# Gate projections in 1024-column blocks, part of them by seven products instead of eight

## The chip, the cores and the metric

The kernel runs on one core of one Trainium2 chip. The metric is the device time of one execution in microseconds (us). TensorE multiplies matrices, VectorE (DVE in the profile) and ScalarE (ACT) work element by element, SyncE (SP) issues the loads and stores; each engine takes its instructions in a fixed order, and they wait for one another by semaphores.

## The reference, cut

One layer of a transformer block for 256 rows of width 2048: three kinds of attention, each with its own branch projection, gates on the branches, an output projection, and a feed-forward part with a short convolution.

```python
h = rms_norm(x, g_mix[l])
proj = h @ w_in[l]
fq, fk, fv, f_logit, sq, sk, sv, mq, gates = jnp.split(proj, cuts, axis=-1)
...            # o_fox, o_sb, o_mem: three attentions over 6, 6 and 4 heads of 128
g = jax.nn.sigmoid(gates.reshape(b, s, N_BRANCH, D_MODEL) + b_gate[l])
merged = (g[:, :, 0] * (o_fox @ w_br_fox[l])
          + g[:, :, 1] * (o_sb @ w_br_sb[l])
          + g[:, :, 2] * (o_mem @ w_br_mem[l]))
x = x + merged @ w_out[l]
h2 = rms_norm(x, g_ffn[l])
u = causal_depthwise_conv(h2 @ w_up[l], conv_w[l], conv_b[l])
u_gate, u_val = jnp.split(u, 2, axis=-1)
x = x + (jax.nn.silu(u_gate) * u_val) @ w_down[l]
```

All inputs are float32. The gates are 3 x 2048 of the columns of `w_in`: a product of 256 x 2048 by 2048 x 6144.

## The kernel before

**Numbers in two parts.** Each float32 operand is held as a rounded part "hi" and a rest "lo". A product is three matmuls (`passes`, L151 to L153, and `three`, L277 to L279): hi by hi, lo of the activations by hi of the weights, hi of the activations by lo of the weights. A piece of weights of 128 x 1024 is loaded into a `raw` tile by SP, copied to `hi` by ScalarE (L140, L272) and split into `lo` by VectorE (L141, L273). `raw` has four buffers (`WBUFS`), `hi` and `lo` four each (`SBUFS`), taken in turn.

**Stages, in order.** The memory's keys and values; projections for the three attentions (mq, f0 to f4, s0 to s4) with the heads' work between them; the gates and branches; the output projection (`o`); the up projection with the convolution (`u`); the down projection (`d`).

**Gates and branches.** The loop at L899 runs over four column blocks `n` of 512. In each, the three gates are projected by `proj` (16 k tiles, two per piece; two row tiles; three matmuls: 96 matmuls a gate), scaled and biased by VectorE straight from PSUM (L910) and passed through the sigmoid (L912); then the three branches are projected by `product` and multiplied in (L924 to L927), and `merged_T` (L877) transposes the merged block for the output projection.

**Eight or seven products.** The output and down projections are made in blocks of 1024 columns by `blocked` (L315), in which a pair of k tiles is a 2 x 2 problem (two row tiles, two column halves, two k tiles). `eight` makes its eight products. `seven` makes seven, in Winograd's manner: it needs sums of the activations (`pair_sums`, L281) and sums of the weights, and adds into four banks `X` and four banks `Y`, which `gather` (L296) puts together on VectorE. A plan string says which pair is done how: "e" by eight, "s" by seven, "f" forms sums of activations. The X and Y banks together are all eight PSUM banks.

**Sums of weights.** They don't depend on the activations, and `weight_sums` (L237) makes them ahead in the background, half a pair at a time: two loads into a tile `pre`, three adds on VectorE (L259 to L261), and a store to DRAM (`kept`), from which `seven` loads them ready made. A half starts every `period` calls of `tick` (one per piece of weights). In the first part of the kernel the period is 7, with the store after 5.

```python
background.append(
    weight_sums(lambda name: gp.tile([P, 1024], F32, tag="pre", bufs=1, name=name), 7, 5, "merged")
)
```

**Order.** TensorE's, ScalarE's and VectorE's order comes from a scheduler, apart from what `keep_in_program_order` fixes. `later` puts a generator of head work, transposes or gathering into a queue, and `tick` runs up to two of them a step further. `xres` holds x for the residual; it is read early for the transposed activations `xT` and the row norms, and again when the output projection is added to it (L303 to L313, L971).

## Time and profile before

| | |
|---|---|
| median of 3 runs | 1474.45 us (1474.35 to 1475.05) |
| span of the profiled execution | 1472.5 us, the only time the page gives of it |
| TensorE busy | 1467.2 us (100%) |
| VectorE busy | 1123.3 us (76%) |
| ScalarE busy | 819.1 us (56%) |
| DMA, mean over the span | 249 GB/s, 367.31 MB |

The profile is of one execution. "PE" is TensorE's matmuls, "PEld" its loads of the stationary operand. A row of a group of instructions has line, engine, operation, tiles written and read, shapes and count, then busy time, mean duration of one in ns, and the idle time of the engine just before them with what ended it. A row of the timeline has start and duration in us. A row of DMA issues ends with size and the median time from issue to landing. A row of a stretch has each engine's busy time with its number of instructions, the granted clock of TensorE, the share of the DMA engines and GB/s. Line numbers are those of the kernel before.

### The profile page before, as it was taken

Reading aid. Unit: us, or ns where it says so; the run is one execution under the profiler, and the core shown is the slowest. Engines: PE = TensorE matmul, PEld = TensorE weight load, DVE = VectorE, ACT = ScalarE, POOL = GpSimd, SP = SyncE. Lnnn points to the kernel's source line nnn. Section 1 sums busy time; section 2 is a strip of 40 time slices with the busy share of each in tenths; the row PEclk is TensorE's granted clock in tenths of the full one; section 3 lists DMA queues with packets and bytes.
Section 4 is the critical chain, followed back from the end, with each engine's and each line's share of the span. In section 5 each row is a group of like instructions: output and inputs, shape, how many; then the busy total and the mean of one; then the engine's idle time right before and its main releaser. Section 6 shows DMA issues by size and latency. Waiting matters only on the chain.

```text
span 1472.5 us, 20543 instructions
## 1 busy us (share of the span) xinstructions
PE 1467.2 (100%) x7373; PEld 1244.8 (85%) x7373; DVE 1123.3 (76%) x1698; ACT 819.1 (56%) x1163; POOL 18.1 (1%) x46
## 2 busy tenths in 40 slices
PE   9999999999999999999999999999999999999999
PEld 7888888888888888888888888888888888888887
DVE  5777666667666657776888899888888777997877
ACT  6755454464544344445666556565566565674664
POOL 0000000011000000000000000000000000000000
PEclk9999999999999999999999999999999999999999
DMA  9685686577788788777758888888885666797796
GB/s 311 203 273 178 206 282 220 172 248 231 239 254 266 247 260 259 245 239 262 251 195 267 288 289 283 281 285 285 285 262 185 198 186 201 242 319 270 258 329 225
DMA packets 213428, 367.31 MB, mean 249 GB/s; under 512 B 13498, under 2 KB 81998, under 8 KB 213326
## 3 DMA queue, kind: packets, MB, share of 16 engines
q1 hardware_dynamic: 211998, 363.90, 76.2%
q10 hardware_dynamic: 1328, 2.11, 0.4%
q8 instruction: 57, 0.93, 0.2%
q14 instruction: 45, 0.37, 0.1%
HBM read 333.44 MB, written 32.51 MB: 249 GB/s over the span
## 4 chain that ended last, share of the span: by engine, by line
PE 99%; DMA 0%; SPq 0%; DVE 0%; ACT 0%; issue 0%; DVEq 0%
PE u L1049 22%; PE u L1050 11%; PE g L151 6%; PE g L153 6%; PE g L152 6%; PE xd L277 4%; PE xd L278 4%; PE xd L279 4%; PE s L151 2%; PE s L153 2%; PE f L151 2%; PE f L153 2%; PE s L152 2%; PE f L152 2%; PE b L152 2%; PE b L151 2%
## 5 line engine op out<-in xcount | busy, mean ns | idle before, releaser
L1049 PE MATMUL u<-hT,hi_u 128*128 128x512 f32 x1232 | 428.4, 391 | 0.0
L1050 PE MATMUL u<-hT,lo_u 128*128 128x256 f32 x1232 | 345.0, 280 | 0.0
L1049 PEld LDWEIGHTS u<-hT,hi_u 128*128 128x128 f32 x1232 | 230.4, 187 | 50.5
L141 DVE TENSOR_TENSOR lo_u<-raw_u,hi_u 128x1024 fp32r<-128x1024 f32 x176 | 215.1, 1222 | 73.1 <-ACT hi_u L140 72.3
L140 ACT CAST hi_u<-raw_u 128x1024 fp32r<-128x1024 f32 x176 | 184.9, 1051 | 137.4 <-PE u L1049 121.0
L1050 PEld LDWEIGHTS u<-hT,lo_u 128*128 128x128 f32 x1232 | 232.8, 189 | 0.0
L141 DVE TENSOR_TENSOR lo_g<-raw_g,hi_g 128x1024 fp32r<-128x1024 f32 x96 | 117.3, 1225 | 78.9 <-ACT hi_g L140 78.3
L140 ACT CAST hi_g<-raw_g 128x1024 fp32r<-128x1024 f32 x96 | 101.0, 1053 | 135.4 <-PE g L152 106.9
L151 PE MATMUL g<-hi_g,xT 128*128 128x512 f32 x336 | 132.0, 393 | 0.0
L153 PE MATMUL g<-lo_g,xT 128*128 128x512 f32 x336 | 130.9, 390 | 0.0
L152 PE MATMUL g<-hi_g,xT 128*128 128x512 f32 x336 | 130.8, 389 | 0.0
L273 DVE TENSOR_TENSOR lo_d<-raw_d,hi_d 128x1024 fp32r<-128x1024 f32 x88 | 106.8, 1222 | 21.1 <-ACT hi_d L272 18.2
L272 ACT CAST hi_d<-raw_d 128x1024 fp32r<-128x1024 f32 x88 | 92.0, 1054 | 49.0 <-PE xd L278 21.4
L153 PEld LDWEIGHTS g<-lo_g,xT 128*128 128x128 f32 x336 | 63.1, 188 | 13.4
L152 PEld LDWEIGHTS g<-hi_g,xT 128*128 128x128 f32 x336 | 63.1, 188 | 12.7
L151 PEld LDWEIGHTS g<-hi_g,xT 128*128 128x128 f32 x336 | 63.1, 188 | 12.7
L140 ACT CAST hi_f<-raw_f 128x1024 fp32r<-128x1024 f32 (+1 forms) x40 | 38.6, 967 | 52.6 <-PE f L152 47.6
L141 DVE TENSOR_TENSOR lo_f<-raw_f,hi_f 128x1024 fp32r<-128x1024 f32 (+1 forms) x40 | 44.7, 1119 | 28.5 <-ACT hi_f L140 26.9
L278 PE MATMUL xd<-hi_d,aT 128*128 128x512 f32 x170 | 66.2, 389 | 0.0
L279 PE MATMUL xd<-lo_d,aT 128*128 128x512 f32 x170 | 66.2, 389 | 0.0
L277 PE MATMUL xd<-hi_d,aT 128*128 128x512 f32 x170 | 66.1, 389 | 0.0
L141 DVE TENSOR_TENSOR lo_s<-raw_s,hi_s 128x1024 fp32r<-128x1024 f32 (+1 forms) x40 | 44.9, 1122 | 27.3 <-ACT hi_s L140 25.2
(422 smaller groups left out, 3029.7 us busy)
## 6 DMA issues: line engine op xcount, KB each, us to landing
raw_u<-in_w_up_dram SPq DMA_DIRECT2D x176, 512.0 KB, 4.5
raw_g<-in_w_in_dram SPq DMA_DIRECT2D x96, 512.0 KB, 4.4
raw_d<-in_w_down_dram SPq DMA_DIRECT2D x66, 512.0 KB, 5.5
pre_d<-in_w_down_dram SPq DMA_DIRECT2D x88, 256.0 KB, 4.8
kept_d<-pre_d SPq DMA_DIRECT2D x44, 512.0 KB, 6.2
raw_f<-in_w_in_dram SPq DMA_DIRECT2D x32, 512.0 KB, 4.2
raw_s<-in_w_in_dram SPq DMA_DIRECT2D x32, 512.0 KB, 4.8
raw_o<-in_w_out_dram SPq DMA_DIRECT2D x25, 512.0 KB, 5.8
```

Source lines behind the costliest of these rows:

```text
L140: pin(nc.scalar.copy(hi[:, :m], raw[:, :m]))
L141: pin(nc.vector.tensor_tensor(lo[:, :m], raw[:, :m], hi[:, :m].bitcast(F32), ALU.subtract))
L151: pin(nc.tensor.matmul(o, lhsT=xh, rhs=wh, start=first, stop=False))
L152: pin(nc.tensor.matmul(o, lhsT=xl, rhs=wh, start=False, stop=False))
L153: pin(nc.tensor.matmul(o, lhsT=xh, rhs=wl, start=False, stop=last))
L272: nc.scalar.copy(hi[:, :n], src)
L273: nc.vector.tensor_tensor(lo[:, :n], src, hi[:, :n].bitcast(F32), ALU.subtract)
L277: nc.tensor.matmul(o, lhsT=ah, rhs=w[0], start=first, stop=False)
L278: nc.tensor.matmul(o, lhsT=al, rhs=w[0], start=False, stop=False)
L279: nc.tensor.matmul(o, lhsT=ah, rhs=w[1], start=False, stop=last)
L1049: nc.tensor.matmul(ps[i], lhsT=hi[:, j, c], rhs=hT(k + j), start=first, stop=False)
L1050: nc.tensor.matmul(ps[i][:, :S], lhsT=lo[:, j, c], rhs=hT(k + j)[:, :S], start=False, stop=last)
```

## The change

The gates are made by `blocked`, in two halves `m` of 1024 columns by three branches, six blocks in all. The first is made by eight throughout. In the other five, three of the eight k pairs are made by seven products. The sums of the weights are not kept in DRAM here: `seven_here` makes them in the raw tiles after their own parts are split off, with four adds of 512 columns, and splits the sums in turn. The sums of the activations, `xs`, are formed for three pairs by `x_sums` behind the forget heads; they lie in the place of `xres`, so x is loaded a second time, behind the first branch weights of the second half. In a block with sevens the bias is added when the Y banks are gathered (`gathered`), with `rneg`, the negated row norm, for subtraction. Both column halves of the three gates are made before the branches of that half. The background's weight sums run with period 4 and store after 3 until the first gate block is done, then with 8 and 3. The matmuls of the gate stage are kept in program order. `merged_T` and `merged_sums` yield a step or more less.

```diff
+    g_plans = (("eeeeeeee", "esesesee", "esesesee"), ("eesessee", "esesesee", "esesesee"))
...
-            for _ in range(period - store):
+            for _ in range(period - store + (slower if "heads" in issued else 0)):
                 yield
...
+        def seven_here(p, first, last):
+            raw0, raw1 = load(2 * p), load(2 * p + 1)
+            (B00,) = parts(raw0[:, :512], f"{name}{nb}_{2 * p}")
+            three(Y[0], *a_of(p, 0, 0), B00, first, last)
+            B10, B11 = parts(raw1, f"{name}{nb}_{2 * p + 1}")
+            three(X[0][0], *a_of(p, 1, 0), B10)
+            three(X[0][1], *f_of(p, FS4), B11)
+            b0, b1 = (raw.rearrange("p (n c) -> p n c", n=2) for raw in (raw0, raw1))
+            nc.vector.tensor_tensor(b0[:, 0], b0[:, 0], b0[:, 1], ALU.add)
+            nc.vector.tensor_tensor(b0[:, 1], b0[:, 1], b1[:, 1], ALU.add)
+            tick()
+            T1w, T3w = parts(raw0, f"t_{name}{nb}_{2 * p}")
+            nc.vector.tensor_tensor(b1[:, 1], b1[:, 1], b0[:, 0], ALU.add)
+            nc.vector.tensor_tensor(b1[:, 0], b1[:, 0], b1[:, 1], ALU.add)
+            three(Y[2], *f_of(p, FS1), T1w, first, last)
+            three(Y[3], *f_of(p, FS3), T3w, first, last)
+            T4w, T2w = parts(raw1, f"t_{name}{nb}_{2 * p + 1}")
+            three(X[1][0], *a_of(p, 1, 1), T4w)
+            three(Y[1], *f_of(p, FS2), T2w, first, last)
+            tick()
...
-        weight_sums(lambda name: gp.tile([P, 1024], F32, tag="pre", bufs=1, name=name), 7, 5, "merged")
+        weight_sums(lambda name: gp.tile([P, 1024], F32, tag="pre", bufs=1, name=name), 4, 3, "merged", slower=4)
...
+    xs = cst.tile([P, GS, 4, 2, P], F32R, tag="xres", name="xs")
+    def x_sums():
+        for p in range(GS):
+            pair_sums(xT.pair(p), block(f"xw_{p}"), [(xs[:, p], slice(0, 4))])
+            yield 2
+    later(x_sums())
...
-    for n in range(4):
-        gate = []
-        for b in range(3):
-            bg = gp.tile([P, 512], F32, tag="bg", name=f"bg_{n}_{b}")
-            nc.sync.dma_start(bg, b_gate[0, b, n0 : n0 + 512].partition_broadcast(P))
-            ps = proj(C_GATE + b * D + n0, 512, f"g{n}_{b}")
-            for t in range(NT):
-                nc.vector.scalar_tensor_tensor(g[:, t], ps[t], rstd[:, t : t + 1], bg, ALU.mult, ALU.add)
+    ordered[0] = True
+    for m in range(2):
+        gate = []
+        for b, plan in enumerate(g_plans[m]):
+            def gathered(n0, Y, m=m, b=b, g=g, bias=bias):
+                ...
+                nc.scalar.copy(e, Y[0])
+                scaled(g[0][:, 0], Y[0], rstd[:, 0:1], 0)
+                nc.vector.tensor_tensor(e, e, Y[1], ALU.add)
+                yield
+                nc.vector.tensor_tensor(f, e, Y[2], ALU.add)
+                scaled(g[1][:, 0], f, rneg[:, 0:1], 1)
+                nc.vector.tensor_tensor(f, e, Y[3], ALU.add)
+                scaled(g[0][:, 1], f, rstd[:, 1:2], 0)
+                yield
+                nc.vector.tensor_tensor(f, f, Y[2], ALU.add)
+                scaled(g[1][:, 1], f, rneg[:, 1:2], 1)
+            X = blocked(
+                "g", w_in, f"{m}{b}", C_GATE + b * D + m * PIECE, plan, lambda p, j: xT(2 * p + j),
+                lambda p, f: xs[:, p, f], raw_g, None, gathered, biases,
+            )
+            for n in range(2):
+                for t in range(NT):
+                    add = g[n][:, t] if "s" in plan else bias[n]
+                    nc.vector.scalar_tensor_tensor(g[n][:, t], X[t][n], rstd[:, t : t + 1], add, ALU.mult, ALU.add)
+            issued.add("heads")
...
+                if (m, n, i) == (1, 0, 1):
+                    xres = cst.tile([P, NT, D], F32, tag="xres", name="xres_again")
+                    for t in range(NT):
+                        nc.sync.dma_start(xres[:, t], xv[:, t])
```

In the text below B00 is the split of a seven's first half tile, B1 that of its second tile, T1/T3 and T4/T2 those of the sums that the adds leave in the first and the second tile.

More of the change, by code (lines that the diff above doesn't have):

```diff
@@ L37 @@
 WINDOW = 2
+GS = 3
 @with_exitstack
@@ L235, in hybrid_block, with weight_sums @@
     )
-    def weight_sums(staging, period, store, end=None, delay=0):
+    def weight_sums(staging, period, store, end=None, delay=0, slower=0):
         for _ in range(delay):
@@ L276, in three @@
     def three(o, ah, al, w, first=False, last=False):
-        nc.tensor.matmul(o, lhsT=ah, rhs=w[0], start=first, stop=False)
-        nc.tensor.matmul(o, lhsT=al, rhs=w[0], start=False, stop=False)
-        nc.tensor.matmul(o, lhsT=ah, rhs=w[1], start=False, stop=last)
+        fix = in_order if ordered[0] else lambda ins: ins
+        fix(nc.tensor.matmul(o, lhsT=ah, rhs=w[0], start=first, stop=False))
+        fix(nc.tensor.matmul(o, lhsT=al, rhs=w[0], start=False, stop=False))
+        fix(nc.tensor.matmul(o, lhsT=ah, rhs=w[1], start=False, stop=last))
     def pair_sums(pair, w, groups):
@@ L383, in seven @@
             tick()
+        def seven_here(p, first, last):
[18 more added lines that the diff above has]
+            tick()
+        by_seven = seven if t4_tile else seven_here
         s, e = 0, ns
@@ L404, in hybrid_block @@
     make_identity(nc, ident)
-    xres = cst.tile([P, NT, D], F32, name="xres")
+    xres = cst.tile([P, NT, D], F32, tag="xres", name="xres")
     xv = x[0].rearrange("(t p) d -> p t d", p=P)
@@ L519, in hybrid_block @@
     ssf = cst.tile([P, NT, 4], F32, name="ssf")
+    rneg = cst.tile([P, NT], F32, name="rneg")
     mix = ctx.enter_context(ExitStack())
@@ L966, in hybrid_block @@
     for nb, plan in enumerate(o_plans):
-        X = blocked("o", w_out, nb, plan, lambda p: mT[p], lambda p, f: ms[p][:, f], raw_o, t4_o[nb], block)
+        X = blocked(
+            "o", w_out, nb, nb * PIECE, plan, lambda p, j: mT[p][:, j], lambda p, f: ms[p][:, f], raw_o, t4_o[nb],
+            lambda n0, Y: gather(n0, Y, block),
+        )
         for n in range(2):
```

85 lines of the change are left out of this document (54 added, 31 removed).

## The prediction

> **What bounds the kernel now.** I read the page's totals and its chain first, then the waits of TensorE, then the chain in order of time for the pitch of its matmuls, then stretches of the gate stage, and last VectorE's timeline and the landings of loads.
>
> ```profile
> span 1472.5 us, 20543 instructions
> PE 1467.2 (100%) x7373; PEld 1244.8 (85%) x7373; DVE 1123.3 (76%) x1698; ACT 819.1 (56%) x1163; POOL 18.1 (1%) x46
> PE 99%; DMA 0%; SPq 0%; DVE 0%; ACT 0%; issue 0%; DVEq 0%
> ...
> PE spare L90 <- DVE qscale L447: 1.2, 1, 1.2
> PE kv L152 <- DVE memT L181: 0.4, 1, 0.4
> ...
> 503.91 0.43 PE mt L885 x4
> 507.12 0.44 PE mt L885 x4
> 591.93 0.44 PE mt L885 x4
> ```
>
> TensorE carries 99% of the chain and in the whole run waits twice, 1.6 us together. So a matmul taken away is time gained, as long as TensorE is still fed. Its price is the pitch, not the 0.39 us that a row shows: between the transposes at 503.91 and those at 591.93 lies one column block of gates and branches, 384 matmuls and 8 transposes of some 0.11 us: (88.02 - 0.88) / 384 = 0.227 us.
>
> ```profile
> core 0: us, PE busy (x) PEld busy (x) DVE busy (x) ACT busy (x) POOL busy (x), PEclk, DMA share, GB/s
> 100.00:125.00 25.00, 25.00 (x116) 20.95 (x115) 18.62 (x34) 13.70 (x24) 0.00 (x0) 1.00 0.76 236
> 275.00:300.00 25.00, 25.00 (x141) 21.51 (x141) 16.03 (x24) 11.87 (x19) 1.73 (x4) 1.00 0.44 127
> 425.00:450.00 25.00, 25.00 (x112) 20.71 (x111) 14.88 (x16) 11.03 (x11) 0.00 (x0) 1.00 0.83 264
> 1275.00:1300.00 25.00, 25.00 (x112) 20.70 (x111) 24.97 (x41) 18.57 (x26) 0.00 (x0) 1.00 0.84 279
> ...
> ACT hi_g L140 <- PE g L152: 106.9, 70, 2.2
> ```
>
> In the gate stage (425 to 450) VectorE is busy 14.9 us of 25, and what ScalarE waits for there is TensorE giving a hi buffer back: the weights are made early. The last row shows that a stage with VectorE busy all the time can still keep TensorE fed (products by seven, in the down projection); but there the sums of weights come ready from DRAM and six raw buffers serve, where the new gates have four and make the sums in place.
>
> **What is gained.** Five blocks have three products by seven each; a seven has 21 matmuls where an eight has 24. 15 x 3 = 45 matmuls x 0.227 = 10.2 us. Everything else on TensorE stays.
>
> **What VectorE gets.** Its price is again a pitch:
>
> ```profile
> 597.13 0.41 DVE L288 TENSOR_TENSOR mw<-mw 128x256 f32<-128x256 f32 x1
> 597.47 1.22 DVE L141 TENSOR_TENSOR lo_g<-raw_g,hi_g 128x1024 fp32r<-128x1024 f32 x1
> ...
> 603.17 0.74 DVE L910 SCALAR_TENSOR_TENSOR g<-g,rstd,bg 128x512 f32<-128x512 f32 x1
> 603.83 0.68 DVE L285 TENSOR_TENSOR mw<-mT 128x512 f32<-128x512 f32 x1
> ...
> 609.42 0.42 DVE L288 TENSOR_TENSOR mw<-mw 128x256 f32<-128x256 f32 x1
> 609.88 0.29 DVE L289 SCALAR_TENSOR_TENSOR mw<-mw 128x128 f32<-128x128 f32 x1
> ...
> 712.05 1.22 DVE L273 TENSOR_TENSOR lo_o<-raw_o,hi_o 128x1024 fp32r<-128x1024 f32 x1
> 713.18 0.68 DVE L312 TENSOR_TENSOR e<-e,yo 128x512 f32<-128x512 f32 x1
> 713.78 0.68 DVE L971 TENSOR_TENSOR xres<-xres,xo 128x512 f32<-128x512 f32 x1
> ```
>
> From start to start a split of 1024 columns takes 1.13 us (712.05 to 713.18), an add of 512 takes 0.60, a scaling 0.66 (603.17 to 603.83), an add of 256 takes 0.34; an op that reads the one before it starts 0.04 behind that one's end (609.88 behind 609.42 + 0.42), so a dependent add costs 0.72. The Trainium skill, VectorE: DVE Perf Modes, section "The DRAIN you can't avoid", says that the next op does not start until the pipe is empty, independent or not. By that, each of some 45 ops of a block would cost 0.08 more, a block 3.5 us, five blocks 17 us more than the sum below; the rows at 712.05 and 713.18 overlap by 0.09, so I go by the rows.
>
> A seven now costs VectorE a split of 512 (0.60), three of 1024 (3.39) and four adds, two of them dependent (2.64): 6.6 us, while TensorE needs 21 x 0.227 = 4.77. An eight costs 2.26 against 5.45. A block (three sevens, five eights) is 19.9 + 11.3, plus gathering the Y banks (four adds, four scalings: 5.0), the last four scalings (2.6) and two halves of the background's weight sums (1.28 each): 41.4 us, against 183 x 0.227 = 41.5 on TensorE. Before, two gate projections of the same work cost it 16 splits, four scalings and two halves, 23.3 us. So the cover is gone: VectorE isn't beyond TensorE, but each time it waits in a block, TensorE soon does too. ScalarE gets 1.5 copies more per seven and stays well below.
>
> **Where it waits.** What stands in line behind VectorE: hi and lo have four buffers in turn, and a seven uses all four in 4.77 us, so the lead shrinks from four pieces of 2.72 to one seven. The second raw tile of a seven is free only after its last split, and in the order "eses" the very same buffer takes the second raw tile of the next seven.
>
> ```profile
> 528.80 0.37 SPq L139 DMA_DIRECT2D raw_g<-in_w_in_dram  x1
> ...
> raw_g<-in_w_in_dram SPq DMA_DIRECT2D x1, 512.0 KB, 4.2
> ...
> 534.24 0.37 SPq L139 DMA_DIRECT2D raw_g<-in_w_in_dram  x1
> ...
> raw_g<-in_w_in_dram SPq DMA_DIRECT2D x1, 512.0 KB, 3.3
> ...
> kept_d<-pre_d SPq DMA_DIRECT2D x1, 512.0 KB, 6.6
> ...
> raw_g<-in_w_in_dram SPq DMA_DIRECT2D x96, 512.0 KB, 4.4
> ...
> L140 ACT CAST hi_g<-raw_g 128x1024 fp32r<-128x1024 f32 x96 | 101.0, 1053 | 135.4 <-PE g L152 106.9 <-PE b L152 20.0 <-issue 3.4
> L912 ACT ACTIVATE g<-g 128x1024 f32<-128x1024 f32 x9 | 9.6, 1063 | 1.5 <-DVE g L910 1.5
> ```
>
> A load by itself (534.24) landed after 3.3 us, one soon behind another (528.80) after 4.2, a store took 6.6, and all 96 have a median of 4.4. Now one block behind another block of sevens. Let TensorE end a block at T; a lo part is wanted with the third of a group's matmuls, 0.45 us into it.
>
> Block start: from the last split of its third seven VectorE has five splits, the gathering and a half: 12.0 us, and TensorE 1.1 + four pieces of 2.72 = 12.0, so both reach T together. Then four scalings (to T + 2.6), the split of the second eight piece (3.8, wanted at 3.2), B00, B1 and the four adds (8.2), T1/T3 (9.3, wanted at 8.55): 1.4 us lost; T4/T2 is split at 10.5 and TensorE leaves the seven at 11.6. Where the order puts the gathering's first scaling ahead of the third seven's last split (two of the three such boundaries), VectorE reaches T 0.66 early and 0.7 is lost.
>
> First to second seven: the buffer is free at 10.5, its load follows another by 1.1 us: 14.7; ScalarE's copy 15.7, then two splits and two adds, 19.3, the copy of T4/T2 20.4, its split 21.6. TensorE, with 8.85 us of work from 11.6 on, wants it at 20.9: 0.7 lost.
>
> Second to third: free at 21.6, load alone 25.0. VectorE itself has two splits, a half, B00 and an add until 26.4, then B1, three adds and two splits: 31.8; TensorE wants T1/T3 at 30.45 and gets it at 30.7: 0.2, or 0.6 where the scaling stands between.
>
> I add 0.4 a block for some four handings-over from one engine to another, an estimate: at 609.88 an op starts 0.04 behind the one it reads on its own engine, and I take 0.1 between engines. So: first seven block of the first half, where ScalarE has two sigmoids (1.06 each) and the last stick-breaking heads ahead of T1/T3: 0.8 + 0.7 + 0.2 + 0.4 = 2.1; the second, 1.4 + 0.7 + 0.6 + 0.4 = 3.1; in the second half the plan "eesessee" has full lead until two sevens stand together, where VectorE needs 8.45 us from the one's last split to the other's and TensorE 4.77 with 0.2 in hand: 3.5; the two behind it 0.7 + 0.7 + 0.6 + 0.4 = 2.4 each. Together 13.5 us. From below it is bounded by 0 (the lead covers all), from above by the loads: with 6.6 instead of 4.2 and 3.3 each of the ten steps from seven to seven costs up to 3 us more.
>
> **What is moved.** Weight sums run every 4 instead of 7 pieces until the gates: 20 instead of 12 halves by then, 8 x 1.28 = 10 us of VectorE over 250 us in which the first two stretches above show 6 to 9 us free of 25, and 8 MB of traffic at shares of 0.44 to 0.76. A load of such a half now stands behind its own store by less than the 6.6 us that the store takes, so SP, with raw loads queued behind, is held up to 4 us; eight buffers of lead cover that, except where pieces are 262 or 256 columns: between 0 and 2 us, I take 0.3. Eight halves fewer in the up projection gain nothing, TensorE sets the end there. The sums of x are three times some 2.4 us on VectorE in the stretch at 275, which has 9 free: nothing. The second x is 2.1 MB on SP's queue ahead of branch weights; at the 264 GB/s of the gate stage this is 8 us of traffic, and a raw tile is asked for when the split of the fourth piece before it ends, 4 x 2.72 - 1.05 - 1.22 = 8.6 us before its own copy, and lands after the 4.4 of the row: between 0 and 3 us, I take 0.3; without that lead it would be the 8.
>
> The sum: 1472.5 - 10.2 + 13.5 + 0.6 = 1476.4 of span. The median of the three runs, 1474.45, lies 1.95 above the profiled span; I keep that distance: 1478.4 us.
>
> **Rivals.** *TensorE stays fed* (ends on the other side): loads land at the 3.3 end and the lead that each block's last eights rebuild covers the block start, so that at most some 7 us are lost: 1464.3 with none, 1471.5 with 7.2. For it: the down projection runs at x112 beside a VectorE that is busy 24.97 of 25. Against: that stage needs no adds in place and has two more raw buffers. It decides at the seven's own cycle: if the last split of a seven follows that of the one before by 10.2 us or less, it holds. Chance 0.27. *Even*: the block starts cost, the steps between sevens don't, 7 to 13 us: 1471.5 to 1477.4. Chance 0.20. *Raw tiles land late*: stores of weight sums, the bias rows and two raw loads share the queues, the landing is nearer to 6.6, and each step costs 1 to 3 us more: 1488 to 1508. Chance 0.09. *The clock falls*: the profile grants 1.00 in all four stretches above, beside no wait longer than 1.2 us. The Trainium skill, TensorE: Matmul & The Clock Gate, section "HAM oscillation — how this bites in real kernels", warns of idle gaps of more than some 3.4 us. My longest wait is under 2 us; if every seven ran at half the clock, 15 x 4.77 us would be added, 1550. Chance 0.01. My forecast, 1477.4 to 1488, has the remaining 0.43.
>
> **The numbers.** 0.2% is 2.9 us, about what a measurement of this kernel can tell from no change: faster 0.27, same 0.20, slower 0.43 + 0.09 + 0.01 = 0.53. The forecast lies near the border of same and slower and cases of both signs are likely, so the range reaches down into the first rival and up to the start of the third: 1465.5 to 1488; the forecast's own range is 1477.4 to 1488.
>
> **What would show it.** TensorE's waits, absent before, should name lo_g and lo_t_g, 0.2 to 2 us each, at T1/T3 and T4/T2 and at the second piece of a block; VectorE should be busy over 90% in the seven blocks; a seven's cycle should be 10.4 to 11.5 us. If TensorE's waits stay under 3 us in all, the first rival is right; if VectorE waits mostly for raw_g to land, the third; if the waits lie before the gates, I was wrong about the moved weight sums.

## The result, and the profile after

The changed kernel takes 1500.70 us (median of 4 runs, 1498.03 to 1502.61) against 1474.40 (4 runs, 1474.23 to 1475.05) for the kernel before on the same chip: a ratio of 1.0176, 95% interval 1.0162 to 1.0191. It is slower, as forecast, but by 26 us where 4 were forecast and the range ended at 13.6. The profiled execution took 1498.03 us, 1.7 more than its span.

The page of the changed kernel: the span, the totals, the first line of the chain.

```profile
span 1496.3 us, 20704 instructions
PE 1470.8 (98%) x7328; PEld 1232.8 (82%) x7328; DVE 1211.8 (81%) x1844; ACT 843.1 (56%) x1201; POOL 18.3 (1%) x46
PE 83%; DVE 8%; DMA 5%; issue 2%; ACT 2%; POOL 0%; SPq 0%; ACTq 0%; DVEq 0%; POOLq 0%
```

45 matmuls are gone (7373 to 7328), and TensorE, which had 99% of the chain, now has 83%: VectorE and loads have come onto it. What TensorE waits for (us in total, times, longest):

```profile
PE z L716 <- POOL sb L859: 5.0, 1, 5.0
PE yg L286 <- DVE lo_t_g L279: 3.0, 5, 0.7
PE xg L284 <- ACT hi_t_g L278: 2.2, 4, 0.8
...
PE xg L286 <- DVE lo_t_g L279: 2.1, 4, 0.5
...
PE yg L284 <- ACT hi_t_g L278: 1.4, 3, 0.9
...
PE xg L286 <- DVE lo_g L279: 1.1, 2, 0.8
```

Four of these rows are the forecast waits, at T1/T3 and T4/T2, and lo_g was forecast too; the five come to 9.8 us. But the largest, z, is at no step of the prediction: it belongs to a stick-breaking head. TensorE's timeline shows the place, the end of the first gate block (start, duration, and in brackets the idle time before):

```profile
361.58 0.39 PE L286 MATMUL xg<-lo_g,xT_rest 128*128 128x512 f32 x1
363.67 0.44 PE L888 MATMUL r<-ls,after_r 128*128 128x384 f32 x1 [1.70 <-ACT ls L883]
...
366.45 0.53 PE L890 MATMUL r<-ls,ones_r 128*128 128x128 f32 x2
372.02 1.22 PE L716 MATMUL z<-sb,vs 128*128 128x256 f32 x2 [5.04 <-POOL sb L859]
...
374.60 0.61 PE L284 MATMUL xg<-hi_g,xT 128*128 128x512 f32 x1
```

Between the last gate matmul of the first block (361.58) and the first of the second (374.60) lie 13 us in which TensorE has only the few matmuls of the last two heads. `blocked` ends with `finish()`, which runs all queued work to its end. Before, `finish()` stood behind the third gate projection, 24 ticks into the gates, when the heads were through; in the changed kernel it stands 16 ticks in, and `x_sums`, queued ahead of the stick-breaking heads, has held one of the two places of the queue for nine ticks. Five ticks of the last two heads are left, and TensorE's order is pinned, so no gate matmul may move up between them. I call this the drain.

In the drain VectorE stands too. Its timeline there:

```profile
360.16 0.69 DVE L265 TENSOR_TENSOR pre_d<-pre_d 128x512 f32<-128x512 f32 x1 [4.79 <-DMA pre_d<-in_w_down_dram]
...
361.57 0.55 DVE L877 TENSOR_TENSOR sb<-sb,z 128x384 f32<-128x384 f32 x1
```

The head's step (L877) stands behind an add of the weight sums (L265) that waits 4.8 us for its load, since VectorE runs in order. Its waits for such loads in the whole run, of which the kernel before has none:

```profile
DVE pre_d L265 <- DMA pre_d<-in_w_down_dram: 19.7, 7, 5.3
DVE pre_o L265 <- DMA pre_o<-in_w_out_dram: 12.6, 8, 3.2
```

To say where the rest went, I measure each stretch from its first matmul to the first of the next, and subtract 0.2267 us for each gate matmul (all_eights below: 192 matmuls in 43.52 us). I also subtract, for the first block, the 9.1 us that the heads' own matmuls take in the kernel before (74.4 us for 288 gate matmuls), and for the fourth block 0.9 for eight transposes. What remains is lost time. Blocks are numbered 1 to 6 in their order; the forecast for them is in the first row. "s" is the length of the stick-breaking projections.

| kernel | time, us | s | 1 | 2 | 3 | 4 | 5 | 6 |
|---|---|---|---|---|---|---|---|---|
| forecast | 1478.4 | 116.5 | 0 | 2.1 | 3.1 | 3.5 | 2.4 | 2.4 |
| before | 1474.4 | 116.2 | - | - | - | - | - | - |
| changed | 1500.7 | 119.2 | 10.4 | 0.7 | 4.3 | 4.3 | 5.8 | 4.1 |
| heads_first | 1489.8 | 118.7 | 2.5 | 1.2 | 4.3 | 4.0 | 5.4 | 4.8 |
| old_period | 1499.0 | 117.1 | 4.3 | 1.1 | 5.7 | 3.5 | 6.4 | 6.4 |
| both | 1492.3 | 116.2 | 0.0 | 1.5 | 5.6 | 4.5 | 6.9 | 7.1 |
| more_raw | 1492.7 | 118.1 | 10.6 | 0.6 | 0.9 | 10.5 | 1.3 | 1.0 |
| heads_raw | 1484.2 | 120.6 | 0.4 | 2.1 | 1.2 | 10.5 | 1.2 | 0.9 |
| all_eights | 1483.3 | 118.2 | 4.6 | 2.2 | 0.0 | 0.1 | 0.0 | 0.0 |
| two_sevens | 1479.9 | 117.4 | 2.8 | 2.1 | 0.2 | 4.7 | 0.8 | 0.2 |
| no_adds | 1472.8 | 117.1 | 4.1 | 1.0 | 0.3 | 2.4 | 0.3 | 0.3 |
| pool_adds | 1524.3 | 116.5 | 1.8 | 8.8 | 10.6 | 13.4 | 11.7 | 9.6 |
| spread_a | 1477.7 | 116.2 | 0.0 | 3.7 | 0.2 | 0.1 | 2.9 | 0.2 |
| spread_b | 1477.2 | 116.2 | 0.0 | 4.3 | 1.2 | 0.1 | 2.2 | 2.0 |
| sums_later | 1501.1 | 119.9 | 4.3 | 1.4 | 6.7 | 3.7 | 8.6 | 4.7 |
| late_a | 1472.0 | 116.2 | 0.0 | 0.3 | 0.2 | 0.1 | 0.2 | 0.2 |
| late_b | 1478.5 | 116.2 | 0.0 | 0.4 | 3.1 | 0.1 | 0.3 | 5.2 |

Times are medians, each against 1474.3 to 1474.6 for before on its own chip; the other columns are from one execution, the profiled one. One execution is a rough measure where weight sums run at the faster rate: heads_first, heads_raw, two_sevens, no_adds and pool_adds give every engine the same instructions up to the first gate block, and yet s is 116.5 to 120.6 us in them, and block 1, which differs at most in its last few instructions, loses 0.4 to 4.1. Where the rate is the old one and the heads end early (both, spread_a, spread_b, late_a, late_b) s is 116.2 each time and block 1 loses nothing.

The span's growth of 23.8 us is then 10.4 (drain), 19.2 (blocks 2 to 6), 3.0 (s) and 1.7 (the two pairs of branches), less the 10.2 saved and less 0.4 that the kernel before loses as well. The 19.2 us are about twice the 9.8 of the wait rows: idle time counts from the end of a matmul's record, 0.39 us behind its start, while the pitch is 0.227, so a wait costs more than its row shows, and the shortest have no row. From the output projection on, the two traces run alike.

Why blocks 3 to 6 lose 18.5 us where 11.4 were forecast is seen in the fifth, on VectorE (L397 and L398 are the first two adds of a seven, L401 and L402 the others):

```profile
563.04 2.50 DVE L279 TENSOR_TENSOR lo_t_g<-raw_g,hi_t_g 128x1024 fp32r<-128x1024 f32 x2
...
568.69 0.69 DVE L279 TENSOR_TENSOR lo_g<-raw_g,hi_g 128x512 fp32r<-128x512 f32 x1 [0.88 <-ACT hi_g L278]
569.41 0.69 DVE L397 TENSOR_TENSOR raw_g<-raw_g 128x512 f32<-128x512 f32 x1
570.68 0.69 DVE L398 TENSOR_TENSOR raw_g<-raw_g,raw_g 128x512 f32<-128x512 f32 x1 [0.57 <-DMA raw_g<-in_w_in_dram]
...
576.65 1.23 DVE L279 TENSOR_TENSOR lo_t_g<-raw_g,hi_t_g 128x1024 fp32r<-128x1024 f32 x1 [1.19 <-ACT hi_t_g L278]
...
583.89 1.23 DVE L279 TENSOR_TENSOR lo_g<-raw_g,hi_g 128x1024 fp32r<-128x1024 f32 x1 [1.28 <-ACT hi_g L278]
...
588.89 1.21 DVE L279 TENSOR_TENSOR lo_t_g<-raw_g,hi_t_g 128x1024 fp32r<-128x1024 f32 x1
```

And on ScalarE, in the same stretch, the copies of the second raw tile, with the copy of T4/T2 between them; then the issues of the two loads that these copies wait for:

```profile
570.68 1.05 ACT L278 CAST hi_g<-raw_g 128x1024 fp32r<-128x1024 f32 x1 [2.03 <-DMA raw_g<-in_w_in_dram]
...
575.57 1.04 ACT L278 CAST hi_t_g<-raw_g 128x1024 fp32r<-128x1024 f32 x1 [2.88 <-DVE raw_g L402]
...
582.81 1.05 ACT L278 CAST hi_g<-raw_g 128x1024 fp32r<-128x1024 f32 x1 [3.64 <-DMA raw_g<-in_w_in_dram]
```

```profile
565.57 0.33 SPq L339 DMA_DIRECT2D raw_g<-in_w_in_dram  x1
...
577.90 0.33 SPq L339 DMA_DIRECT2D raw_g<-in_w_in_dram  x1
```

The last split of one seven ends at 565.54, that of the next at 577.88, that of the third at 590.10: cycles of 12.3 and 12.2 us, where 10.2 keeps TensorE fed. VectorE is the engine in demand and yet stands in each cycle: for a load (0.57), or for a copy of ScalarE's that waits for a load (0.88, 1.28), and the load of a second raw tile waits for the buffer that the last split has just freed. The wait of 1.19 is of another kind: the copy at 575.57 waits for VectorE's own last add (L402), and the split waits for that copy. Both loads are issued as soon as the buffer is free; the copy at 570.68 starts 5.1 us after the split that freed it, and the one at 582.81 4.9 us.

### The profile page after: what moved, and what is told of

The parts are those of the page before. It is cut to its first block, busy times and chain, and to the rows that moved or that the text cites. A ratio compares the mean times of both kernels' runs of the same rounds, so it can differ in the third digit from the quotient of the medians.

```text
span 1496.3 us, 20704 instructions
## 1 busy us (share of the span) xinstructions
PE 1470.8 (98%) x7328; PEld 1232.8 (82%) x7328; DVE 1211.8 (81%) x1844; ACT 843.1 (56%) x1201; POOL 18.3 (1%) x46
## 4 chain that ended last, share of the span: by engine, by line
PE 83%; DVE 8%; DMA 5%; issue 2%; ACT 2%; POOL 0%; SPq 0%; ACTq 0%; DVEq 0%; POOLq 0%
PE u L1131 22%; PE u L1132 11%; PE xd L284 4%; PE xd L286 4%; PE xd L285 4%; DMA raw_g<-in_w_in_dram 2%; PE f L284 2%; PE f L286 2%; PE f L285 2%; PE b L286 2%; PE xg L286 2%; PE xg L284 2%; PE xg L285 2%; PE b L284 2%; PE b L285 2%
## 5 line engine op out<-in xcount | busy, mean ns | idle before, releaser
L1132 PE MATMUL u<-hT,lo_u 128*128 128x256 f32 x1232 | 341.4, 277 | 0.0
L141 ACT CAST hi_u<-raw_u 128x1024 fp32r<-128x1024 f32 x176 | 184.7, 1050 | 136.7 <-PE u L1131 117.4
L278 ACT CAST hi_g<-raw_g 128x1024 fp32r<-128x1024 f32 (+1 forms) x96 | 92.7, 982 | 75.4 <-DMA raw_g<-in_w_in_dram 45.9
L279 DVE TENSOR_TENSOR lo_g<-raw_g,hi_g 128x1024 fp32r<-128x1024 f32 (+1 forms) x96 | 108.2, 1139 | 12.5 <-ACT hi_g L278 12.2
L286 PE MATMUL xg<-lo_g,xT 128*128 128x512 f32 x231 | 90.4, 391 | 1.1 <-DVE lo_g L279 1.1
L284 PE MATMUL xg<-hi_g,xT 128*128 128x512 f32 x231 | 90.9, 394 | 0.0
L285 PE MATMUL xg<-hi_g,xT 128*128 128x512 f32 x231 | 90.0, 390 | 0.0
L1131 PE MATMUL u<-hT_rest,hi_u 128*128 128x512 f32 x176 | 62.1, 393 | 0.0
L141 ACT CAST hi_s<-raw_s 128x1024 fp32r<-128x1024 f32 (+1 forms) x40 | 38.4, 961 | 40.9 <-PE s L285 25.7
L1103 ACT ACTIVATE y<-u,taps 128x256 f32<-128x256 f32 x88 | 49.2, 595 | 14.7 <-DVE u L1100 14.7
L142 DVE TENSOR_TENSOR lo_f<-raw_f,hi_f 128x1024 fp32r<-128x1024 f32 (+1 forms) x40 | 44.4, 1117 | 15.2 <-ACT hi_f L141 13.5
```

The lines of the kernel that those rows point to most:

```text
L141: pin(nc.scalar.copy(hi[:, :m], raw[:, :m]))
L142: pin(nc.vector.tensor_tensor(lo[:, :m], raw[:, :m], hi[:, :m].bitcast(F32), ALU.subtract))
L278: nc.scalar.copy(hi[:, :n], src)
L279: nc.vector.tensor_tensor(lo[:, :n], src, hi[:, :n].bitcast(F32), ALU.subtract)
L284: fix(nc.tensor.matmul(o, lhsT=ah, rhs=w[0], start=first, stop=False))
L285: fix(nc.tensor.matmul(o, lhsT=al, rhs=w[0], start=False, stop=False))
```

## The experiments

**The drain.** In heads_first the sums of x are made beside the queue, and each head waits a tick less; one tick of heads is left instead of five.

```diff
-            yield 2
+            yield
+            yield
+            yield
...
-    later(x_sums())
+    background.append(x_sums())          # ahead of the projection s3
...
-        yield 2
+        yield 1
         yield from until("vs0", "vs1")
```

> The changed kernel with the sums of x made beside the heads' queue instead of in one of its two places, and one tick less wait in each stick-breaking head, so that one tick of heads instead of five is left when the first gate block ends. Theory A (10.5 of the 34 us that were lost over the expected gain lie in that drain, where TensorE has only the heads' few matmuls): the gap before the second gate block's first matmul shrinks from 13.0 to some 3 us, about 10 us less, 1488 to 1492 us. Rival B (the drain is long because VectorE stands 4.8 us for a load of the moved weight sums, and that wait goes wherever the heads go): at most 5 us less, 1495 to 1498.

1489.81 us (1488.59 to 1494.04), 10.9 less, theory A's number. The trace is of the slowest of the four executions: block 1 loses 2.5 instead of 10.4, s and blocks 2 to 6 in sum are as they were to 0.5 us, and the branches take 2.1 us more, the stages ahead of s 1.8. So the early end of the heads takes back 7.9 us of the drain there. In old_period the weight sums run at their old rate:

```diff
-  ... 4, 3, "merged", slower=4)
+  ... 7, 5, "merged")
```

> The changed kernel with the background's weight sums at their old rate (a half every 7 pieces to the end, store after 5) and nothing else undone. Theory B (VectorE's waits for the loads of the weight sums, 32 us in the changed kernel and none before, cost TensorE 3.0 us in the stick-breaking projections and 4.8 in the drain): 1491 to 1494 us, and the rows of VectorE waiting for these loads are gone. Rival A (the drain alone, its length set by the heads' own chain): the 3.0 us of the projections at most, 1497 to 1498.

1498.98 us (1495.86 to 1499.66): 1.7 less, close to the rival's number, but not for its reason. VectorE's waits for these loads are gone, and as theory B said s and the drain get shorter, by 2.1 and 6.1 us. The sevens' blocks and the branches took 6 of the 8 us again. From the second block to the output projection 16 halves of weight sums now start instead of 13, which may be why; it was not tried by itself. The drain's 10.4 us don't split into two prices: the old rate alone takes 6.1 off, the early end of the heads 7.9, the two together all of it, since the heads' steps stand behind the sums' adds.

> The two edits together: old rate of the weight sums, and the heads ended before the first gate block does. If the two are separate causes, the gains add up: 1484 to 1488 us, and what is left over before plus the 10.2 us that the sevens save, about 20 us, lies in the blocks with sevens. If they are one and the same wait, it is no better than the better one of the two.

1492.29 us (1491.52 to 1493.08), no better than heads_first: s and block 1 lose nothing any more, and blocks 3 to 6 lose 24.1 instead of 18.5. The two edits clear the front; the gain is given back behind.

In early_finish the kernel before alone gets the early end:

```diff
             for t in range(NT):
                 nc.vector.scalar_tensor_tensor(g[:, t], ps[t], rstd[:, t : t + 1], bg, ALU.mult, ALU.add)
+            if (n, b) == (0, 1):
+                finish()
```

> The kernel before with one line more: what is left of the heads is ended behind the second gate projection of the first column block (16 ticks in) instead of the third (24 ticks in), which leaves three ticks of heads to run through at once. If ending the heads early is what costs, 3 of the changed kernel's 5 ticks should cost 4 to 7 us: 1478 to 1482 us. Rival: it costs only because the changed kernel also pins TensorE's order, so that no gate matmul may move up between the heads' matmuls; before leaves them free, and the third projection fills the gaps: under 1 us, 1474 to 1475.5.

1476.10 us, ratio 1.0009 (0.9999 to 1.0018), nearer the rival: the first three gates take 76.0 us instead of 74.4. Ending the heads early costs little by itself. It has three ticks, not five, and no pinned order; which of the two makes the difference from old_period's 4.3 was not told apart.

**Sevens or blocks.** all_eights takes the sevens out and leaves the rest.

```diff
-    g_plans = (("eeeeeeee", "esesesee", "esesesee"), ("eesessee", "esesesee", "esesesee"))
+    g_plans = (("e" * 8,) * 3,) * 2
```

> The changed kernel with all products by eight: 1024-column blocks, the heads' drain, the faster weight sums, the sums of x (unused) and the second load of x stay, the sevens and their 10.2 us of savings go. If the drain (10.5 us) and the waits of the stick-breaking projections (3.0) are all that the rest of the change costs: 1487 to 1491 us, and blocks behind the first take 43.6 to 44 us each. Rival: blocks of 1024 columns lose time of their own at each start (four result banks freed at once): 1.5 us for each of six blocks more, 1496 to 1500.

1483.31 us (1482.11 to 1483.90), ratio 1.0059: a little better than expected, and the rival falls: blocks 3 to 6 lose nothing, so the blocks of 1024 columns are free. s, the drain and block 2 lose 2.0, 4.6 and 2.2 us here. The changed kernel is 17.4 us slower than this one. Its sevens lose 16.9 us more in blocks 2 to 6 and save 10.2, which makes 6.7; the rest lies in the drain (5.8), the branches and s, and these differ although the edit leaves them alone. One difference is the second load of x: nothing reads the sums of x in all_eights, so it is issued in s already, at 294 us, and not at 645.

**The raw ring.** more_raw takes a seven's second raw tile from the pool of 4 KB blocks.

```diff
-            raw0, raw1 = load(2 * p), load(2 * p + 1)
+            raw0 = load(2 * p)
+            raw1 = block(f"raw_{name}{nb}_{2 * p + 1}")
+            nc.sync.dma_start(raw1, wv[:, 2 * p + 1, n0 : n0 + PIECE])
```

> The changed kernel, but the second raw tile of every seven is taken from the pool of 4 KB blocks (several free there) instead of the ring of four, so that its load no longer waits for the last split of the seven before. Theory C (a seven's cycle of 12.2 us is buffer freed, load of about 5 us, copy, splits and adds in turn): the cycle falls to 10.5 us or less and the five blocks lose some 8 to 12 us less, 1489 to 1493 us. Rival D (VectorE's own work, 41 us a block beside TensorE's 41.5, sets it): VectorE is already busy 22 to 24 of 25 us, so at most 3 us less, 1497 to 1500.

1492.69 us (1490.30 to 1493.42), 8.0 less: theory C's number. In block 5 the last split of a seven now follows that of the one before by 9.2 and 10.5 us, and blocks 3, 5 and 6 lose 0.9 to 1.3 instead of 4.1 to 5.8. But block 4 loses 6 us more. VectorE there (L176 is the split of the merged rows for the output projection):

```profile
508.40 0.69 DVE L399 TENSOR_TENSOR raw_g<-raw_g 128x512 f32<-128x512 f32 x1
513.74 0.69 DVE L176 TENSOR_TENSOR mT<-mt,mT 128x512 fp32r<-128x512 f32 x1 [4.65 <-ACT mT L175]
516.96 0.69 DVE L176 TENSOR_TENSOR mT<-mt,mT 128x512 fp32r<-128x512 f32 x1 [2.52 <-ACT mT L175]
```

These splits stand in VectorE's order between the first and the second add of a seven, and VectorE waits 7.2 us for them with the seven's work behind. heads_raw has both edits:

> The edits of heads_first and more_raw together. If the drain of the heads and the ring of raw tiles are two separate causes, their gains add up (about 10 and 7 us): 1481 to 1485 us, and blocks with sevens take some 42.7 us where VectorE is busy all the time. Rival: the earlier loads stand in the heads' way or the other way round, and only the better of the two is left: 1488 to 1491.

1484.23 us (1482.23 to 1488.37), as expected for two causes: 16.5 of 18.9 us add up. no_adds asks whether what its steady blocks still lose is VectorE's own work; it leaves out the four adds:

```diff
-            nc.vector.tensor_tensor(b0[:, 0], b0[:, 0], b0[:, 1], ALU.add)
-            nc.vector.tensor_tensor(b0[:, 1], b0[:, 1], b1[:, 1], ALU.add)
...
-            nc.vector.tensor_tensor(b1[:, 1], b1[:, 1], b0[:, 0], ALU.add)
-            nc.vector.tensor_tensor(b1[:, 0], b1[:, 0], b1[:, 1], ALU.add)
```

> The kernel heads_raw without the four adds of each seven (the products then use unsummed weights, so the gate values are not the reference's); loads, copies, splits and matmuls stay. VectorE's work of a block falls from 41.4 to 33.5 us. Theory D (with enough buffers a block's length is VectorE's work): the second, fifth and sixth blocks' 42.4 to 42.7 us go to 41.5 to 41.8, and the run is 2 to 5 us shorter than heads_raw: 1479 to 1482.5. Rival (handings-over from engine to engine, or late loads): 42.4 and more each, 1483 to 1485.

The stretches of blocks 5 and 6, of heads_raw and then of no_adds (bounds, length, busy time of PE, PEld, DVE, ACT, POOL, granted clock, DMA share, GB/s):

```profile
550.50:593.20 42.70, 42.14 (x184) 34.20 (x183) 42.21 (x54) 23.42 (x26) 0.00 (x0) 1.00 0.75 254
593.20:635.60 42.40, 42.10 (x185) 34.31 (x184) 41.91 (x53) 23.90 (x26) 0.00 (x0) 1.00 0.74 251
```

```profile
539.90:581.70 41.80, 41.80 (x185) 34.36 (x184) 34.32 (x41) 23.75 (x26) 0.00 (x0) 1.00 0.79 265
581.70:623.50 41.80, 41.80 (x185) 34.35 (x184) 34.22 (x41) 24.18 (x26) 0.00 (x0) 1.00 0.77 261
```

VectorE is busy 42.21 of 42.70 us with the adds and 34.32 without: 7.9 us, the forecast's price of twelve adds. The blocks fall to 41.80, as theory D said. Without the adds the chain from copy to add to copy is shorter too, so this run doesn't part work from chain; that VectorE stands only 0.5 us of 42.7 in heads_raw speaks for the work. The run is 1472.76 us (1470.13 to 1473.84), 11.5 less than heads_raw where 2 to 5 were expected: 8.1 of it is block 4, where the adds stand among the splits of the merged rows.

pool_adds moves the four adds to GpSimd (`nc.vector` to `nc.gpsimd` in these lines):

> The kernel heads_raw with the four adds of each seven on GpSimd, which has nothing else to do there. Theory D: VectorE's work of a block falls from 41.4 to 33.5 us, TensorE is fed again, and the blocks go to 41.5 to 42.3 us each: 1474 to 1479 us. Rival: an add takes GpSimd over 2 us (no add of this kernel runs there, so no row shows it) or slows VectorE beside it, and since the chain add, add, copy, split lies between a tile's arrival and its product, the seven's cycle grows: 1485 us and more.

1524.34 us (1522.24 to 1524.49), 40 more than heads_raw: the rival. The groups of GpSimd's adds (count, busy time, mean ns):

```profile
L399 POOL TENSOR_TENSOR raw_g<-raw_g 128x512 f32<-128x512 f32 x15 | 32.6, 2172 | 183.1 <-DVE lo_g L279 155.6 <-DMA kept_d<-pre_d 18.8 <-DMA raw_g<-in_w_in_dram 8.6
L400 POOL TENSOR_TENSOR raw_g<-raw_g,raw_g 128x512 f32<-128x512 f32 x15 | 19.6, 1310 | 7.6 <-DMA raw_g<-in_w_in_dram 6.6
```

An add takes 1.3 to 2.2 us there and 0.68 on VectorE, and it lies in the chain between a tile's arrival and its product; unloading the busy engine made the chain longer.

two_sevens is heads_raw with the plans "eseeseee", and "eeseesee" in block 4:

> The kernel heads_raw with two sevens a block instead of three, none of them side by side (ten in all, 6.8 us of matmuls saved instead of 10.2). Theory D (once the buffers serve, VectorE's 41 to 42 us of work set a block's length): VectorE gets 37.1 us a block and TensorE 186 x 0.227 = 42.2, so each block goes down to 42.2 to 42.8, and the block that had two sevens side by side (54.9 us with its transposes in more_raw) gains most: 1473 to 1478 us. Rival: each seven costs a fixed 1 us of handings-over, whatever VectorE's load: 1479 to 1483.

1479.88 us (1477.57 to 1480.26), above the expected 1473 to 1478. Blocks 3, 5 and 6 do what theory D says (0.2 to 0.8 lost), and so the fixed price of the rival falls; block 4 still loses 4.7. Block 1 loses 2.8 where heads_raw, with the same instructions up to there, lost 0.4.

**Do the sevens pay?** spread_a and spread_b have the old rate, the ended heads, the block pool, block 4 by eight, and "eseeseee" or "esesesee" in blocks 2, 3, 5 and 6.

> Heads ended before the first gate block does, second raw tile of a seven from the block pool, weight sums at the old rate, and eight sevens: two in each of four blocks, none side by side, none in the block behind the first pair of branches. 24 matmuls fewer than before, 5.4 us. By the blocks of two_sevens (lost 0.2 to 2.1 us each beside 0.2267 a matmul) some 3 us are lost: 1471 to 1473.5 us, a little faster than before. Rival: the weight sums at the old rate leave a half more in each gate block, and VectorE's waits for them stop the sevens as in the run both: 1474.5 to 1477.

> As spread_a, with three sevens in each of the four blocks: 36 matmuls fewer, 8.2 us. By the blocks of heads_raw (lost 0.9 to 2.1 us each) some 5.5 us are lost: 1471 to 1474 us, the same as spread_a within 1 us, since the third seven of a block saves 0.7 us and takes VectorE over TensorE's time by as much. Rival: as in both, 1476 and more.

1477.69 (1475.86 to 1479.83) and 1477.20 us (1474.80 to 1478.52): the rivals' numbers, or just above. s, block 1 and block 4 are clean, blocks 3 and 6 nearly so, but blocks 2 and 5 lose 2 to 4 us. VectorE in spread_a's block 2, then in its block 5:

```profile
366.46 0.69 DVE L265 TENSOR_TENSOR pre_d<-pre_d 128x512 f32<-128x512 f32 x1 [3.37 <-DMA pre_d<-in_w_down_dram]
...
367.99 1.22 DVE L279 TENSOR_TENSOR lo_g<-raw_g,hi_g 128x1024 fp32r<-128x1024 f32 x1
```

```profile
543.29 0.69 DVE L400 TENSOR_TENSOR raw_g<-raw_g,raw_g 128x512 f32<-128x512 f32 x1 [2.35 <-DMA raw_g<-in_w_in_dram]
```

In block 2 a weight-sum add stands in front of a split that TensorE wants. In block 5 it is not that: there the first seven's second raw tile lands late. The next runs went after the weight sums. sums_later puts these adds two ticks behind their load, in the changed kernel:

```diff
+            for _ in range(2):
+                yield
             both = w[:, 1:2].to_broadcast([P, 2, 256])
...
-            for _ in range(store):
+            for _ in range(store - 2):
```

> The changed kernel with the adds of the background's weight sums put two ticks behind their load (rate and store as they are), so that VectorE doesn't stand for that load. If that standing makes the drain long and the waits of the stick-breaking projections: the first gate block goes from 63.0 us to 56 to 59, those projections from 119.2 to 116.5 us, and the run to 1490 to 1495 us. Rival (the drain is only the five ticks of heads, the sums' waits are covered): 1498 us or more, as in old_period.

1501.13 us (1500.39 to 1501.89): no gain. Block 1 did what the theory said (56.9 us; 4.3 lost instead of 10.4), s did not, and blocks 2 to 6 lose 25.1 instead of 19.2. Among SyncE's waits over blocks 3 to 6 (400 to 650 us) the store's (L272) has grown; L270 is the same store in the changed kernel:

```profile
SPq L272 <- DVE pre_d L269: 22.4, 5, 5.8
```

```profile
SPq L270 <- DVE pre_d L267: 4.1, 6, 0.9
```

With the adds closer to their store, the store waits on SyncE for VectorE, 22.4 us instead of 4.1, and the raw loads queued behind it wait with it. best_a, best_b and best_d carried that edit (with 3 ticks) over to spread_a, spread_b and a variant with two late sevens in block 4, and loaded the bias rows at a block's last seven.

> spread_a (two sevens in each of four blocks) with the adds of the weight sums three ticks behind their load and the bias rows loaded at a block's last seven instead of its first, so that the load of the weight sums isn't held behind a bias load that waits for its buffer. If VectorE's standing for that load is what costs 3 us at the first seven of each half: the second and fifth blocks go from 45.9 and 45.0 us to 43, and the run to 1471 to 1474 us, at or below before. Rival (the first seven's own chain, or ScalarE's sigmoids ahead of its copies, costs the 3 us): 1475.5 to 1478 as spread_a.

> spread_b (three sevens in each of four blocks) with the same two edits as best_a. By the same reason 1470 to 1473.5 us, within 1 us of best_a; by the rival 1475 to 1478.

> best_a with two sevens more, late in the block behind the first pair of branches (four eights first, so that the splits of the merged rows on VectorE are done by then): 6 matmuls fewer, 1.4 us. If a seven with buffers and VectorE time costs nothing: 1470 to 1473 us, 1 us below best_a. Rival: that block lost 4.7 us with early sevens because the merged rows' splits stand among the sevens' adds, and will again: 1475 us and more.

1497.40 (1490.36 to 1501.93), 1492.86 and 1495.26 us, all missed: the edit also reaches the weight sums of the up projection, where the store waits behind the convolution's steps on VectorE. best_a there, between 780 and 1150 us:

```profile
SPq L272 <- DVE y L1117: 36.3, 7, 5.9
```

So their totals say nothing of the gates. Their gate blocks do: block 2 of best_a loses 2.1 instead of 3.7, block 5 2.2 instead of 2.9, but block 6 1.5 instead of 0.2. In best_d block 4, its sevens behind four eights, loses 0.3 where two_sevens lost 4.7, but block 5 then loses 5.1. The first seven's place is what late_a tries. It leaves the weight sums as in spread_a, and moves the sevens one eight back and the bias loads to the last seven:

```diff
+    g_plans = (("eeeeeeee", "eeseesee", "eeseesee"), ("eeeeeeee", "eeseesee", "eeseesee"))
...
-                if s == 0 and ready:
+                if s == ns - 1 and ready:
                     ready()
```

> spread_a with each block's two sevens one eight later (two eights ahead of them) and the bias rows loaded at a block's last seven. If the 3.7 and 2.9 us that the second and fifth blocks lost come from the first seven's place behind the sigmoids, the scalings and the held load of weight sums: each block loses under 1 us, so 5.4 saved less some 2: 1470 to 1473 us, faster than before by 0.1 to 0.3%. Rival (any first seven loses its 2 us, since its chain load, copy, split, adds, copy, split is longer than the lead, or the block's end now lacks lead for the gathering): 1474.5 to 1477.5.

1471.97 us (1470.49 to 1472.30, 11 runs) against 1474.55: ratio 0.9980 (0.9971 to 0.9989), 0.2% faster than the kernel before, as expected. Its four blocks with sevens (2, 3, 5, 6), and all of TensorE's waits in the run:

```profile
361.96:404.47 42.51, 42.51 (x190) 35.00 (x188) 37.03 (x48) 23.00 (x26) 0.00 (x0) 1.00 0.74 248
404.47:446.84 42.37, 42.37 (x187) 34.92 (x186) 37.94 (x47) 22.13 (x23) 0.00 (x0) 1.00 0.74 246
535.81:578.19 42.38, 42.38 (x188) 34.91 (x186) 36.60 (x45) 22.18 (x24) 0.00 (x0) 1.00 0.80 263
578.19:620.56 42.37, 42.37 (x187) 34.91 (x186) 37.93 (x47) 21.18 (x22) 0.00 (x0) 1.00 0.77 259
```

```profile
PE spare L91 <- DVE qscale L477: 1.2, 1, 1.2
PE b L286 <- DVE lo_b L142: 0.9, 1, 0.9
PE kv L153 <- DVE memT L184: 0.4, 1, 0.4
```

VectorE is busy 36.6 to 37.9 of 42.4 us, and TensorE waits for nothing in the gates. That free time is not enough by itself: in spread_a, with the same sevens at other places, VectorE is as free (37.5 us busy in block 2), and blocks 2 and 5 lost 3.7 and 2.9. late_a moves the sevens and the bias loads at once; which of the two did it was not told apart. 5.4 us are saved there and 2.6 arrive. Of the rest, 1.5 us lie in the second pair of branches (46.0 instead of 44.5 us). x is loaded again there, but it is in spread_a too, whose branches take 44.5; which load is late was not tried.

> late_a with three sevens a block (two eights first, one last): 8.2 us saved. By the same reason some 1 to 1.5 us lost in each block, where VectorE's 41.4 us meet TensorE's 41.5: 1470 to 1473 us. Rival: with one eight at a block's end the gathering and the next block's start fall on VectorE together, 2 us a block more: 1475 to 1479.

1478.48 us (1475.99 to 1480.52): the rival. With a third seven and one eight at the end, blocks 3 and 6 lose 3.1 and 5.2 us at their start, where TensorE waits for lo_g, the first split behind the gathering.

## Why the prediction was right or wrong

**The gain, right.** 45 matmuls are gone, and all_eights shows the pitch at 0.2267 us: 10.2.

**VectorE's prices, right.** A block at 41.4 us with adds of 2.64 a seven: heads_raw shows VectorE busy 41.9 to 42.2, and leaving out the adds takes 7.9 off. Had each op cost 0.08 us more than the overlapping rows say, a block would have kept it busy for some 45.

**The first failed step: "Everything else on TensorE stays".** I costed what the change adds to VectorE and did not ask what the new `finish()` at the end of `blocked` releases. I wrote of the last stick-breaking heads only as work ahead of T1/T3 on ScalarE. The drain of 10.4 us, of which heads_first takes back 7.9 and the run both all, is the largest single loss and was in neither the sum nor a rival.

**The second: the steps from seven to seven, 0.7 and 0.2 us.** The mechanism was right: VectorE's wait becomes TensorE's, at the places named, and the ring of raw tiles sets the cycle, as more_raw shows. The size was off. I took the load to be issued when the buffer is free, which holds, and to land after 4.2 and 3.3 us; the copy starts 5.1 and 4.9 us after the freeing split. By my own times the cycles in block 5 would have been 11.1 and 10.2 us; they were 12.3 and 12.2. The loads came 0.9 and 1.5 us later than I took them; the rest lies in the chain behind them. Meanwhile VectorE, in order, stands for what is late (0.9, 0.6 and 1.3 us in the rows above) instead of doing the next seven's work. The blocks lost 19.2 instead of 13.5: 18.5 instead of 11.4 in blocks 3 to 6, but 0.7 instead of 2.1 in block 2, which follows the drain. The rival "raw tiles land late" (0.09), with landings nearer to 6.6 us, put 1488 to 1508 on this and holds the measured time, but half by accident: without the drain and s the result would have been some 1487 us, inside my range.

**The third: the moved weight sums at 0.3.** I bounded them by SyncE's hold, between 0 and 2 us. Nothing bounded VectorE: its in-order adds wait for the loads, 32 us in the run and none before. In the profiled executions the old rate gives TensorE 2.1 us back in s and 6.1 in the drain. The sentence "if the waits lie before the gates, I was wrong about the moved weight sums" is what happened. The second load of x, forecast at 0.3, is not to blame for the 1.7 us that the branches lose: 1.1 lie in the first pair, where x isn't loaded, and in heads_raw and spread_a, which load x before the second pair too, both pairs run in 44.5 us, as if nothing were lost.

**The signs.** VectorE was to be busy over 90% in the seven blocks. Of the five blocks with sevens it is in two: 92% in blocks 3 and 6, but 86 to 89% in blocks 2, 4 and 5. Block 5, with its edges rounded to 1 us:

```profile
555.00:602.00 47.00, 43.64 (x183) 33.47 (x182) 41.95 (x53) 23.29 (x25) 0.00 (x0) 1.00 0.72 235
```

The rival "TensorE stays fed" was to decide at a cycle of 10.2 us, and it was not met; late_a, with two sevens a block, buffers of their own and two eights ahead, keeps TensorE fed.

## What to carry to other kernels

When a helper is used in a new place, cost everything that it calls, the closing drain above all: queued side work needs main work beside it, and pinned order forbids the main work to help. When an engine becomes as loaded as the one that bounds, leave it a tenth in hand, and look where its bursts fall: 37 to 38 us of 42.4 ran without a wait in late_a and lost up to 3.7 in spread_a; at 42 us no kernel here ran without loss. In-order queues turn each wait for a load into a wait for all behind it; moving that wait from VectorE to a store on SyncE only moved the loss.

## What was not expected of the hardware

The granted clock fell behind shorter waits of TensorE than I thought of. The drain of the changed kernel, just before the fall and during it, then the same two stretches in block 4 of more_raw:

```profile
361.30:364.60 3.30, 1.44 (x6) 0.73 (x6) 3.04 (x8) 0.71 (x2) 1.59 (x4) 1.00 0.35 137
364.70:374.80 10.10, 4.75 (x16) 3.62 (x15) 7.53 (x12) 3.04 (x6) 2.47 (x4) 0.50 0.47 139
```

```profile
539.70:543.00 3.30, 1.43 (x5) 0.90 (x6) 3.23 (x4) 2.84 (x3) 0.00 (x0) 1.00 0.00 0
543.10:546.40 3.30, 3.30 (x9) 2.57 (x8) 2.71 (x4) 2.45 (x4) 0.00 (x0) 0.50 0.69 206
```

```profile
PE yg L284 <- ACT hi_t_g L278: 1.8, 1, 1.8
```

In the drain the clock is at 0.50 from 364.7 us on, behind a wait of 1.7 us (to 363.67); the wait of 5.0 (from 367.0 to 372.0) comes only after that. In more_raw the longest wait of a gate matmul in the whole run is 1.8 us, the last row, and yet the clock is halved for over 3 us; half of some 3.3 us, 1.7 us by this estimate, is lost each time. heads_raw shows the same at the same place, and block 4 of either run contains it. In both stretches before a fall TensorE was busy some 1.4 of the 3.3 us. The Trainium skill, TensorE: Matmul & The Clock Gate, section "HAM oscillation — how this bites in real kernels", gives idle gaps of more than some 3.4 us as what throttles. Neither fall agrees, as no wait ahead of them is longer than 1.8 us. Nor is the longest wait alone what decides: in block 6 of the kernel named both, a wait of 2.6 us left the clock at 1.00. What does decide stays open.

```profile
596.39 0.50 PE L286 MATMUL xg<-lo_g,xT 128*128 128x512 f32 x1 [2.59 <-DVE lo_g L279]
```

```profile
596.40:602.00 5.60, 5.60 (x25) 4.64 (x26) 5.50 (x8) 1.23 (x2) 0.00 (x0) 1.00 0.84 268
```
